# A KV-cache copy cut in two: half rows of 1,984 B in place of packets of 63 KB

## The chip, the cores and the metric

The kernel runs on one core of a Trainium2 chip. A core has five engines that run their own instruction streams: TensorE (PE, matmuls), VectorE (DVE), ScalarE (ACT), GpSimd (POOL) and SyncE (SP). Data moves between HBM and the on-chip memory, or within HBM, by DMA: an engine issues a transfer into its own queue, and sixteen DMA engines that all queues share carry it out. The metric is the time of one execution on the device, in microseconds (us).

## The reference

One layer of a decoder: 512 prompt tokens and 8 sequences of 4 new tokens each. A combined input projection feeds a convolution branch and an attention branch with three groups of key/value (KV) windows; then come an output projection, a layer norm, a feed-forward network (FFN) and a second layer norm. For the 8 sequences the reference also returns each group's KV window, moved on by 4 tokens:

```python
WINDOWS = (128, 512, 2048)
...
cat = jnp.concatenate([kv_prev[g].astype(kv_new.dtype), kv_new], axis=1)
o, lse = dilated_attn_sample(q, cat[:, :, 0], cat[:, :, 1], DILATIONS[g], slopes)
new_kv.append(cat[:, T:])
```

So 124 of 128, 508 of 512 and 2,044 of 2,048 old tokens of every sequence, 4 KB each, are copied from an input to an output without any arithmetic.

## The kernel before, in words

All activations are held with channels on the 128 partitions and the 544 tokens (512 and 32) along the row, in two halves of 272. Every projection is a stream of weight tiles: `load_more` (L109 to L117) has SP load a tile `wr` into one of four buffers, `prep_to` splits it into a high and a low part (a cast on ACT, L131, to `wh`, and a subtraction on DVE, L132, to `wl`), and `mm_group` (L189 to L200) runs three matmuls for each 128 channels and half (L194, L195, L197). The order of the instructions on each engine is the order in which the program writes them; other work (convolution, attention) is written as generators that `tick` advances between the matmul groups. SP is not held to that order by hand, but it too issues its transfers one after the other, and one that must wait holds all behind it.

The program goes through the first projections, four rounds of query/key/value projections (one for each pair of heads, `hp` 0 to 3), the gates with the branch projections, the output projection, and the FFN in three parts. The attention of a pair of heads lags a round behind its projections. Its last step, `combine_gen` (L554), turns a small table of softmax sums round through HBM: SP stores `st` to `dx` in HBM (L557, 8 KB, 128 pieces of 64 B) and loads it back as `stn` (L558). The load waits on SP until the store has landed.

At the start of the attention of the next pair, PE transposes the values into PSUM (`vtp`), ACT copies them out (`vT`, L473), and the score matmuls `S` (L486, L488) use the same PSUM buffers after that.

The KV copies are pieces in a list, `cp_pieces` (L167 to L178): for each sequence four pieces of the largest cache (out `s2`), one of the middle one (`s1`), and after every fourth sequence one piece for four sequences of the smallest (`s0`). ACT issues the next piece (L186) each time that `copies` has been called often enough: in the query/key/value rounds (L647) and in the first two and the third part of the FFN (L1073, L1079). These places in ACT's order are called slots here; what is left in the list is issued at L1099.

Transfers that SP and ACT issue take turns in the use of eight completion semaphores; an instruction that issues a transfer can therefore wait for an older one.

Of the kernel before, what the change touches and what calls it, by code (L numbers as in the profile page):

```python
# [54 lines left out]
def hybrid_step_kernel(ctx: ExitStack, tc: tile.TileContext, I, O):  # L55
# [33 lines left out]
    def C(name):  # L89
        o, w = CST[name]  # L90
        return cst[:, o:o + w]

    def big_tile(i, shape, dt, name):
        return big.tile(shape, dt, tag=f"L{i}", name=name)

    # ---------------------------------------------------------------- weight stream
    stream = []
    done = []
    pos = {"load": 0, "prep": 0, "use": 0, "free": 0}
# [58 lines left out]
        for m in range(8):  # L158
            add_w(I["w_down"][m, :, k0:k1, :], k1 - k0, None if j < 2 else (f"wd{m // 4}", f"wd{m // 4}", m % 4))

    # ---------------------------------------------------------------- background work
    bg = []

    def tick():
# [4 lines left out]
    cp_pieces = []  # L169
    for b in range(NB):  # L170
        for h in range(4):
            cp_pieces.append((O["s2"][b].rearrange("(p a) -> p a", p=128)[:, h * 4088:(h + 1) * 4088],
                              I["c2"][b, 4096:].rearrange("(p a) -> p a", p=128)[:, h * 4088:(h + 1) * 4088]))
        cp_pieces.append((O["s1"][b].rearrange("(p a) -> p a", p=128),
                          I["c1"][b, 4096:].rearrange("(p a) -> p a", p=128)))
        if b % 4 == 3:
            cp_pieces.append((O["s0"][b - 3:b + 1].rearrange("b (p a) -> b p a", p=128),
                              I["c0"][b - 3:b + 1, 4096:].rearrange("b (p a) -> b p a", p=128)))  # L178
    cp_acc = [0.0]

    def copies(n):
# [3 lines left out]
            o, i = cp_pieces.pop(0)  # L185
            act.dma_start(out=o, in_=i)  # L186

    # ---------------------------------------------------------------- matmul groups
    def mm_group(w, A, nk, halves=(0, 1)):  # L189
        hi, lo = w  # L190
        ps = {h: pmm.tile([128, 512], F32, tag="mm", name="mm") for h in halves}
        for k in range(nk):
            for h in halves:
                pe.matmul(ps[h][:, :HC], lhsT=hi[:, k], rhs=A[h][:, 0, k], start=(k == 0), stop=False)  # L194
                pe.matmul(ps[h][:, :HC], lhsT=hi[:, k], rhs=A[h][:, 1, k], start=False, stop=False)  # L195
            for h in halves:
                pe.matmul(ps[h][:, :HC], lhsT=lo[:, k], rhs=A[h][:, 0, k], start=False, stop=(k == nk - 1))  # L197
            if len(halves) == 2 and nk > 4 and k == nk // 2 - 1:
                tick()
        return ps  # L200

    # ---------------------------------------------------------------- setup
    ct = const.tile([128, 8, 9], F32, name="ct")
    csg = const.tile([128, 8, 9], F32, name="csg")
    cpad = const.tile([128, 8, 32], F32, name="cpad")
# [35 lines left out]
        act.copy(out=A[:, 0, ks, 240:], in_=src)  # L241
        dve.tensor_tensor(out=A[:, 1, ks, 240:], in0=src, in1=A[:, 0, ks, 240:].bitcast(F32), op=ALU.subtract)

    # ---------------------------------------------------------------- first modulation, u, first projections
    U = [big_tile(h, [128, 2, 8, HC], F32R, f"u{h}") for h in range(2)]

    def ada_mm(g):
# [61 lines left out]
    early_mm(2)  # L309
    dve.tensor_scalar(out=qb, in0=V("b_in", 0, 60), scalar1=0.125, scalar2=None, op0=ALU.mult)  # L310

    # ---------------------------------------------------------------- the other modulation parts
    aslots = (3, 4, 5, 6, 3, 4, 6, 4)
    abox = {}

# [36 lines left out]
                    out=modT[:, part, q0:q0 + 4, :], in0=pt[:, :, 32 * j:32 * j + 9],  # L352
                    scalar=0.0 if part == 3 else 1.0, in1=bias, op0=ALU.add, op1=ALU.add)

    # ---------------------------------------------------------------- GLU
    glu = big_tile(2, [128, 4 * 542 + 4 * NB * 34 + NS * CW], F32, "glu")
    glu_p = glu[:, :4 * 542].rearrange("p (c t) -> p c t", c=4)
    glu_s = glu[:, 4 * 542:4 * 542 + 4 * NB * 34].rearrange("p (c b t) -> p c b t", c=4, b=NB)
# [35 lines left out]
    pool.dma_start(out=O["conv_s"], in_=glu_s.rearrange("p c b t -> p (c b t)"))  # L394
    pool.dma_start(out=O["conv_p"], in_=glu_p[:, :, 512:542])

    # ---------------------------------------------------------------- layer norm (channel-major)
    def ln_core(z, nk, scratch, width, wait):
        acc = tmp.tile([128, HC], F32, tag="ln", name="lnacc")
        dve.tensor_reduce(out=acc, in_=z.rearrange("p k n -> p n k"), axis=AX.X, op=ALU.add)  # L400
        for _ in range(wait):
            yield
        ps = ps_o.tile([128, 512], F32, tag="o", name="lnps")
        pe.matmul(ps[:, :HC], lhsT=ones, rhs=acc, start=True, stop=True)
        mean = ps[:, :HC].unsqueeze(1).to_broadcast([128, 2, HC])
        for k in range(0, nk, 2):
            zz = z[:, k:k + 2]
            dve.scalar_tensor_tensor(out=zz, in0=mean, scalar=-1.0 / width, in1=zz, op0=ALU.mult, op1=ALU.add)
            act.activation(out=scratch[:, k:k + 2], in_=zz, func=AF.Square)
        acc2 = tmp.tile([128, HC], F32, tag="ln", name="lnacc2")  # L410
        dve.tensor_reduce(out=acc2, in_=scratch.rearrange("p k n -> p n k"), axis=AX.X, op=ALU.add)
        for _ in range(wait):
            yield
        ps2 = ps_o.tile([128, 512], F32, tag="o", name="lnps2")
        pe.matmul(ps2[:, :HC], lhsT=ones, rhs=acc2, start=True, stop=True)
        sd = tmp.tile([128, HC], F32, tag="ln", name="lnsd")
        act.activation(out=sd, in_=ps2[:, :HC], func=AF.Sqrt, scale=1.0 / width, bias=epst[:, 0:1])
        dve.reciprocal(out=sd, in_=sd)
        return sd

    # ---------------------------------------------------------------- conv branch
    box = {}

    def conv_gen():
# [35 lines left out]
            yield  # L460
        box["Y"] = [Y[:, 0], Y[:, 1]]

    # ---------------------------------------------------------------- prompt attention
    att = []
    dist = C("dist")

# [132 lines left out]
        split_rows(oa[:, HC:], att[1], hp, 0, 240)  # L599
        yield  # L600

    # ---------------------------------------------------------------- qkv projections
    conv = conv_gen()
    chain = []
    idle = [False]
# [48 lines left out]
    pool.dma_start(out=O["ks"], in_=smp[:, :, 3 * NS:])  # L654
    pool.dma_start(out=O["vs"], in_=smv.rearrange("p c b n -> p c (b n)"))

    # ---------------------------------------------------------------- decode attention
    dect = C("dect")

    live = {}  # L660
# [1 line left out]
    def load_k(b):  # L662
        KT = big_tile(5, [128, 9, 4, 132], F32, "KT")
        for g in range(3):
            sp.dma_start(out=KT[:, 3 * g:3 * g + 3], in_=I["kt"][b, :, 3 * g:3 * g + 3])
        live["k", b] = KT
# [110 lines left out]
        act.copy(out=att[1][:, 0, :, 240:], in_=as32)  # L777
        dve.tensor_tensor(out=att[1][:, 1, :, 240:], in0=as32, in1=att[1][:, 0, :, 240:].bitcast(F32), op=ALU.subtract)

    # ---------------------------------------------------------------- gates and branch projections  # L780
    load_k(0)
    chain.append(attn_gen(3, qk, 2, lambda: load_v(0), decode_gen))
    idle[0] = True
# [4 lines left out]
    for m in range(8):  # L788
# [5 lines left out]
        for h in range(2):  # L794
            hs = slice(h * HC, (h + 1) * HC)
# [30 lines left out]
    for m in range(8):  # L826
        ps = mm_group(w_next(), att, 4)
        mg = tmp.tile([128, NT], F32, tag="w", name="mg")
        for h in range(2):
            hs = slice(h * HC, (h + 1) * HC)  # L830
# [16 lines left out]
    for m in range(0, 8, 2):  # L847
        sp.dma_start(out=z[:, m:m + 2], in_=I["x_t"][:, m:m + 2])

    # ---------------------------------------------------------------- output projection, LN1, u2  # L850
    res["wo1"] = [big_tile(i, [128, 4, 8, 128], F32R, f"wo1{i}") for i in (2, 3)]
    flags.add("wo1")
    def bt(ap):
# [2 lines left out]
    u2 = {}  # L856
# [111 lines left out]
    for h in range(2):  # L968
        stats = Stats(h, dve if h else pool)
        for m in range(8):  # L970
# [12 lines left out]
            if h == 1:  # L983
                a = tmp.tile([128, NS], F32, tag="w", name="zsa")
# [12 lines left out]
        bg.append(ln1_gen(h, stats))  # L997
        tick()

    # ---------------------------------------------------------------- FFN  # L1000
    def gu_evict(pg, pu, Hs, fi):
        hs = list(pg)
        sg = {}
        for h in hs:
            sg[h] = tmp.tile([128, HC], F32, tag="w", name="sgf")
            act.activation(out=sg[h], in_=pg[h][:, :HC], func=AF.Sigmoid)
        for h in hs:
            dve.tensor_tensor(out=sg[h], in0=sg[h], in1=pg[h][:, :HC], op=ALU.mult)
        for h in hs:
            dve.tensor_tensor(out=sg[h], in0=sg[h], in1=pu[h][:, :HC], op=ALU.mult)  # L1010
        for h in hs:
            act.copy(out=Hs[h][:, 0, fi], in_=sg[h])  # L1012
        for h in hs:
            dve.tensor_tensor(out=Hs[h][:, 1, fi], in0=sg[h], in1=Hs[h][:, 0, fi].bitcast(F32), op=ALU.subtract)
# [25 lines left out]
    for j, (k0, k1) in enumerate(FF_CHUNKS):  # L1040
# [3 lines left out]
        if j == 0:  # L1044
            gw = [w_next(1) for _ in range(4)]
            first = []
# [191 lines left out]
```

## Time and profile before

| | |
|---|---|
| median of 3 runs | 1056.1 us |
| lowest, highest | 1054.32, 1061.54 us |
| profiled execution, from first to last instruction | 1060.8 us |
| PE busy | 1008.7 us, 95% of the span |
| data moved by DMA | 242.64 MB |
| of it by ACT's queue, mostly KV copies | 88.43 MB in 5,640 packets |
| copies issued by ACT | 32 of 2,044 KB, 8 of 2,032 KB, 2 of 1,984 KB |

The profile is one execution, traced on the chip; its own time is given as that span alone. It lies 4.7 us above the median of the runs. In the rows below, an instruction carries the line of the kernel that made it, and its names stand as out<-in. PE is a matmul, PEq, ACTq and SPq are an engine's instruction queue (there a transfer is issued). q1 is the DMA queue of SP, q10 that of ACT, q0 that of POOL. "[11.44 <-ACT vT L473]" means that the engine stood idle for 11.44 us before the instruction and that the named one ended the wait. PEclk is the granted clock of TensorE as a share of the full one.

### The profile page before, as it was taken

The numbers are of one execution on the slowest core, as the hardware profiler recorded it, in microseconds if no ns is written. First come the engines' busy times: TensorE is split into PE (matmuls) and PEld (weight loads), VectorE is DVE, ScalarE is ACT, GpSimd is POOL, SyncE is SP. The second block draws the span as 40 slices with busy tenths as digits, with TensorE's granted clock in tenths as the row PEclk, the third lists the DMA queues.
The fourth block names the chain that finished last, engine by engine and source line by source line (L and its number), as shares of the span: only waits on it lengthen the run. The fifth ranks groups of instructions, "written<-read, shape, count | busy, mean of one in ns | idle before, by whom it ended". The sixth has DMA issues, their size and how long they took to land.

```text
span 1060.8 us, 21530 instructions
## 1 busy us (share of the span) xinstructions
PE 1008.7 (95%) x9168; PEld 966.8 (91%) x9168; DVE 564.5 (53%) x988; ACT 415.9 (39%) x798; POOL 154.4 (15%) x226
## 2 busy tenths in 40 slices
PE   4999999999999959999999989999999999999995
PEld 3887999999988958999999989999999999999994
DVE  3422788789786335343216868633433434434487
ACT  3312235445448438544433445522212322223333
POOL 0201010010004400111103565100000000000046
PEclk8999999999999989999999999999999999999998
DMA  9898688796785664599953620457765677744202
GB/s 380 332 389 318 232 300 288 243 341 236 267 300 183 269 207 155 177 381 394 371 210 97 237 80 21 135 191 263 254 233 175 228 245 256 250 172 152 82 24 85
DMA packets 42951, 242.64 MB, mean 229 GB/s; under 512 B 7400, under 2 KB 8680, under 8 KB 35624
## 3 DMA queue, kind: packets, MB, share of 16 engines
q1 hardware_dynamic: 34592, 126.83, 33.8%
q10 hardware_dynamic: 5640, 88.43, 22.9%
q0 software_dynamic: 2624, 26.02, 6.1%
q8 instruction: 72, 1.18, 0.4%
q14 instruction: 23, 0.19, 0.0%
HBM read 231.36 MB, written 97.58 MB: 310 GB/s over the span
## 4 chain that ended last, share of the span: by engine, by line
PE 77%; DVE 8%; DMA 6%; POOL 3%; ACT 3%; issue 2%; ACTq 0%; DVEq 0%; SPq 0%; POOLq 0%
PE mm L194 22%; PE mm L195 22%; PE mm L197 21%; DMA dx<-st 3%; PE od L735 2%; PE Sd L700 2%; PE adaps L329 1%; DMA wr<-in_w_in 1%; DVE mrg L824 1%; PE pt L511 1%; POOL z L978 1%; DVE wl L132 1%; DMA wr<-in_w_pc 1%; DMA cst<-in_cst 1%; DVE z L1029 1%
## 5 line engine op out<-in xcount | busy, mean ns | idle before, releaser
L194 PE MATMUL mm<-u,wh 128*128 128x272 f32 x1528 | 419.7, 292 | 0.0
L195 PE MATMUL mm<-u,wh 128*128 128x272 f32 x1528 | 412.5, 288 | 0.0
L197 PE MATMUL mm<-u,wl 128*128 128x272 f32 x1528 | 317.9, 288 | 0.0
L194 PEld LDWEIGHTS mm<-u,wh 128*128 128x128 f32 x1528 | 288.0, 188 | 14.2 <-issue 11.0
L195 PEld LDWEIGHTS mm<-u,wh 128*128 128x128 f32 x1528 | 287.9, 188 | 0.2
L132 DVE TENSOR_TENSOR wl<-wr,wh 128x1024 fp32r<-128x1024 f32 (+2 forms) x132 | 155.3, 1178 | 171.4 <-ACT wh L131 171.4
L197 PEld LDWEIGHTS mm<-u,wl 128*128 128x128 f32 x1528 | 239.7, 188 | 0.0
L131 ACT CAST wh<-wr 128x1024 fp32r<-128x1024 f32 (+2 forms) x132 | 130.5, 991 | 178.2 <-PE mm L195 129.0
L434 DVE SCALAR_TENSOR_TENSOR convy<-glu,vec,convy 128x512 f32<-128x512 f32 x120 | 95.6, 797 | 2.5
L195 PE MATMUL mm<-h,wh 128*128 128x272 f32 x240 | 64.8, 288 | 0.0
L194 PE MATMUL mm<-h,wh 128*128 128x272 f32 x240 | 64.5, 287 | 0.0
L1012 ACT CAST h<-sgf 128x272 fp32r<-128x272 f32 x44 | 17.0, 420 | 103.2 <-DVE sgf L1010 103.2
L894 POOL TENSOR_TENSOR lnq<-lnq,lnsq 128x272 f32<-128x272 f32 x4 | 3.1, 775 | 365.7 <-ACT lnsq L868 365.7
L1019 DVE SCALAR_TENSOR_TENSOR z<-mm,modT,z 128x272 f32<-128x272 f32 (+1 forms) x48 | 21.7, 479 | 55.4 <-PE mm L197 55.4
L1010 DVE TENSOR_TENSOR sgf<-sgf,mm 128x272 f32<-128x272 f32 x44 | 17.5, 434 | 63.3 <-PE mm L197 63.0
L197 PE MATMUL mm<-h,wl 128*128 128x272 f32 x240 | 49.6, 288 | 0.0
L632 ACT ACTIVATE qk<-mm,vec 128x272 f32<-128x272 f32 (+1 forms) x48 | 25.8, 625 | 56.6 <-PE mm L197 56.6
L194 PEld LDWEIGHTS mm<-h,wh 128*128 128x128 f32 x240 | 45.2, 188 | 0.0
L195 PEld LDWEIGHTS mm<-h,wh 128*128 128x128 f32 x240 | 45.2, 188 | 0.0
L504 ACT ACTIVATE P<-P,st 128x256 f32<-128x256 f32 x64 | 31.2, 489 | 28.6 <-DVE st L498 25.7
L195 PE MATMUL mm<-mrg,wo 128*128 128x272 f32 x128 | 37.8, 295 | 1.8 <-DVE mrg L824 1.7
L194 PE MATMUL mm<-mrg,wo 128*128 128x272 f32 x128 | 38.3, 300 | 0.0
(270 smaller groups left out, 1632.2 us busy)
## 6 DMA issues: line engine op xcount, KB each, us to landing
out_s<-in_c ACTq DMA_DIRECT2D x32, 2044.0 KB, 9.0
wr<-in_w_in SPq DMA_DIRECT2D x60, 512.0 KB, 6.3
wr<-in_w_gu SPq DMA_DIRECT2D x44, 512.0 KB, 4.3
KT<-in_kt SPq DMA_DIRECT2D x24, 792.0 KB, 7.5
VV<-in_vv SPq DMA_DIRECT2D x24, 768.0 KB, 7.4
gb<-in_w_ada POOLq DMA_DIRECT2D x8, 2048.0 KB, 16.8
out_s<-in_c ACTq DMA_DIRECT2D x8, 2032.0 KB, 8.9
ga<-in_w_ada SPq DMA_DIRECT2D x8, 1024.0 KB, 12.0
```

Source lines behind the costliest of these rows:

```text
L131: act.copy(out=hv, in_=raw)
L132: dve.tensor_tensor(out=lv, in0=raw, in1=hv.bitcast(F32), op=ALU.subtract)
L194: pe.matmul(ps[h][:, :HC], lhsT=hi[:, k], rhs=A[h][:, 0, k], start=(k == 0), stop=False)
L195: pe.matmul(ps[h][:, :HC], lhsT=hi[:, k], rhs=A[h][:, 1, k], start=False, stop=False)
L197: pe.matmul(ps[h][:, :HC], lhsT=lo[:, k], rhs=A[h][:, 0, k], start=False, stop=(k == nk - 1))
L434: dve.scalar_tensor_tensor(out=o, in0=src, scalar=sc, in1=o, op0=ALU.mult, op1=ALU.add)
L504: act.activation(out=p[:, a:b], in_=p[:, a:b], func=AF.Exp, bias=st[:, kd, s, hh, 0:1], accum_out=st[:, kd, s, hh, 1:2])
L632: act.activation(out=o, in_=src, func=AF.Identity, bias=V("b_in", col))
L700: pe.matmul(S[32 * c:32 * c + 32, 132 * g:132 * g + 132], lhsT=q[:, col:col + 32], rhs=KT[:, j, c], start=(t == 0), stop=(j == 0 or t == 3))
L735: pe.matmul(o[32 * c:32 * c + 32, :], lhsT=lhsT, rhs=rhs, start=(j == 0), stop=(j == 9))
L1010: dve.tensor_tensor(out=sg[h], in0=sg[h], in1=pu[h][:, :HC], op=ALU.mult)
L1019: dve.scalar_tensor_tensor(out=zz[:, :n1], in0=ps[:, :n1], scalar=modT[:, 5, m, 0:1], in1=zz[:, :n1], op0=ALU.mult, op1=ALU.add)
```

## The change

The piece for four sequences of the smallest cache becomes two pieces. Each sequence's 124 tokens are seen as 128 rows of 992 numbers (3,968 B); the first piece copies the first 496 numbers of each row (1,984 B), the second the rest. Nothing else in the program changes (the diff also empties some comment lines, and moves the later lines down by two).

```diff
         if b % 4 == 3:
-            cp_pieces.append((O["s0"][b - 3:b + 1].rearrange("b (p a) -> b p a", p=128),
-                              I["c0"][b - 3:b + 1, 4096:].rearrange("b (p a) -> b p a", p=128)))
+            for h in range(2):
+                hs = slice(h * 496, (h + 1) * 496)
+                cp_pieces.append((O["s0"][b - 3:b + 1].rearrange("b (p a) -> b p a", p=128)[:, :, hs],
+                                  I["c0"][b - 3:b + 1, 4096:].rearrange("b (p a) -> b p a", p=128)[:, :, hs]))
```

The list has 44 pieces in place of 42. Three places of ACT's order show what that moves. A row is line, operation, out<-in and shape; `out_s0`, `out_s1` and `out_s2` are the copies, and the shape of a copy is the pattern of its destination, slowest count first, in numbers of 4 B. The tiles `qk3` are the projections of the last pair of heads, `P` and `PT` its attention, `convy` and `yconv` the convolution.

In the last round of projections, ACT before the change:

```order
L630 ACTIVATE qk3_3135<-mm_3618,qb_100 128x68x4
L630 ACTIVATE qk3_3135<-mm_3619,qb_100 128x60x4
L186 DMA out_s0<-in_c0 4x8x15872
L514 COPY PT_3712<-pt_3707 128x512
L409 ACTIVATE convy_1064<-convy_1064 128x2x272 x2
L131 CAST wh_3722<-wr_3331 128x1024
```

and with the change:

```order
L632 ACTIVATE qk3_3135<-mm_3618,qb_100 128x68x4
L632 ACTIVATE qk3_3135<-mm_3619,qb_100 128x60x4
L188 DMA out_s0<-in_c0 512x1x496
L516 COPY PT_3712<-pt_3707 128x512
L411 ACTIVATE convy_1064<-convy_1064 128x2x272 x2
L131 CAST wh_3722<-wr_3331 128x1024
```

The first copy of the smallest cache, 4 x 8 runs of 15,872 numbers, becomes its first half, 512 runs of 496, in the same slot.

The next two slots, at the end of that round and into the gates, before:

```order
L630 ACTIVATE qk3_3135<-mm_3809,qb_100 128x272
L630 ACTIVATE qk3_3135<-mm_3810,qb_100 128x240
L186 DMA out_s2<-in_c2 128x4088
L455 ACT_TABLE_LOAD
L455 ACTIVATE convy_1064<-convy_1064 128x4x272
L131 CAST wh_3877<-wr_3545 128x512
L534 COPY osb_3505<-o_3909 128x2x128
L458 CAST yconv_3241<-convy_1064 128x1088
L632 ACTIVATE qk3_3135<-mm_3883,vec_95 128x272
L632 ACTIVATE qk3_3135<-mm_3884,vec_95 128x240
L186 DMA out_s2<-in_c2 128x4088
L131 CAST wh_3961<-wr_3616 128x1024
```

and with the change:

```order
L632 ACTIVATE qk3_3135<-mm_3809,qb_100 128x272
L632 ACTIVATE qk3_3135<-mm_3810,qb_100 128x240
L188 DMA out_s0<-in_c0 512x1x496
L457 ACT_TABLE_LOAD
L457 ACTIVATE convy_1064<-convy_1064 128x4x272
L131 CAST wh_3877<-wr_3545 128x512
L536 COPY osb_3505<-o_3909 128x2x128
L460 CAST yconv_3241<-convy_1064 128x1088
L634 ACTIVATE qk3_3135<-mm_3883,vec_95 128x272
L634 ACTIVATE qk3_3135<-mm_3884,vec_95 128x240
L188 DMA out_s2<-in_c2 128x4088
L131 CAST wh_3961<-wr_3616 128x1024
```

The second half takes the slot of a copy of the largest cache; that copy moves to the next slot, and each later piece by one slot. Behind the second of these slots stand the cast of a weight tile and then the `vT` copies.

In the third part of the FFN (`sgf`, `h20`, `h21` are its activations), before:

```order
L1012 CAST h21_10200<-sgf_10564 128x272
L186 DMA out_s0<-in_c0 4x8x15872
L131 CAST wh_10575<-wr_10329 128x1024
L131 CAST wh_10631<-wr_10385 128x1024
L1006 ACTIVATE sgf_10687<-mm_10581 128x272
L1006 ACTIVATE sgf_10689<-mm_10582 128x272
L1012 CAST h20_10199<-sgf_10687 128x272
L1012 CAST h21_10200<-sgf_10689 128x272
L131 CAST wh_10699<-wr_10454 128x1024
```

and with the change:

```order
L1014 CAST h21_10200<-sgf_10564 128x272
L188 DMA out_s1<-in_c1 32x16256
L131 CAST wh_10575<-wr_10329 128x1024
L131 CAST wh_10631<-wr_10385 128x1024
L1008 ACTIVATE sgf_10687<-mm_10581 128x272
L1008 ACTIVATE sgf_10689<-mm_10582 128x272
L1014 CAST h20_10199<-sgf_10687 128x272
L1014 CAST h21_10200<-sgf_10689 128x272
L188 DMA out_s0<-in_c0 512x1x496
```

The list now ends two slots later: the last copy of the smallest cache stood in the first of these slots, where now the last of the middle cache stands; its halves stand in the second of these slots and in the one after it.

## Rows read from the trace of the kernel before

**Rows 1.** Of the page, part 1: busy time, share of span, instructions

```profile
PE 1008.7 (95%) x9168; PEld 966.8 (91%) x9168; DVE 564.5 (53%) x988; ACT 415.9 (39%) x798; POOL 154.4 (15%) x226
```

**Rows 2.** Waits of all engines, whole span: who, for whom, us, times, longest

```profile
PE S L486 <- ACT vT L473: 11.4, 1, 11.4
...
PE adaps L251 <- DVE cpad L228: 6.7, 1, 6.7
```

**Rows 3.** Chain that ended last, 336 to 400 us: start, us, what

```profile
343.72 37.12 DMA dx<-st
...
381.33 7.87 DMA wr<-in_w_pc
389.21 0.63 ACT wh L131
```

**Rows 4.** Waits of SP's queue, whole span

```profile
SPq L558 <- DMA dx<-st: 42.3, 4, 36.6
```

**Rows 5.** Tile dx, whole span: time to landing

```profile
DMA to landing us min/median/max: 1.4/3.0/37.1
```

**Rows 6.** SP in order of time, 335 to 395 us: start, us, what

```profile
342.96 0.66 SPq L115 DMA_DIRECT2D wr<-in_w_in  x1
343.72 0.43 SPq L557 DMA_DIRECT2D dx<-st  x1
380.86 0.38 SPq L558 DMA_DIRECT2D stn<-dx  x1
```

**Rows 7.** ACT in order of time, 336 to 398 us

```profile
342.14 1.19 ACTq L186 DMA_DIRECT2D out_s<-in_c  x1
...
356.13 0.56 ACTq L186 DMA_DIRECT2D out_s<-in_c  x1
...
363.56 0.83 ACT L632 ACTIVATE qk<-mm,vec 128x272 f32<-128x272 f32 x2
...
380.01 1.04 ACT L131 CAST wh<-wr 128x1024 fp32r<-128x1024 f32 x1 [15.62 <-DMA wr<-in_w_in]
380.96 1.55 ACT L473 COPY vT<-vtp 128x512 f32<-128x512 f32 x3
```

**Rows 8.** PE in order of time, 366 to 403 us

```profile
382.08 1.49 PE L486 MATMUL S<-qk 64*128 64x128 f32 x7 [11.44 <-ACT vT L473]
```

**Rows 9.** Stretches: window, length, PE busy (count), granted clock, DMA share, GB/s

```profile
370.60:382.00 11.40, 0.04 (x1) 0.73 0.46 171
382.00:386.00 4.00, 3.92 (x20) 0.50 1.02 399
386.00:390.00 4.00, 4.00 (x34) 0.99 0.87 256
```

**Rows 10.** DMA queues, 352 to 356 us: packets, MB, share of 16 engines

```profile
q10 hardware_dynamic: 5, 0.32, 18.3%
q1 hardware_dynamic: 5, 0.03, 1.5%
```

**Rows 11.** DMA queues, 359.4 to 362.5 us

```profile
q10 hardware_dynamic: 60, 1.22, 102.1%
```

**Rows 12.** DMA packets by size, 349 to 352 us

```profile
DMA packets 234, 0.91 MB, mean 304 GB/s; under 512 B 127, under 2 KB 127, under 8 KB 226
```

**Rows 13.** DMA packets by size, 377 to 380.5 us

```profile
DMA packets 107, 0.27 MB, mean 77 GB/s; under 512 B 52, under 2 KB 52, under 8 KB 102
```

**Rows 14.** DMA queues, first 22 us

```profile
q10 hardware_dynamic: 576, 0.74, 9.2%
```

**Rows 15.** Of the page, part 3: queue totals

```profile
q1 hardware_dynamic: 34592, 126.83, 33.8%
```

**Rows 16.** The same, around the second copy of the smallest cache

```profile
955.00:980.00 25.00, 25.00 (x201) 1.00 0.44 159
```

**Rows 17.** PE's waits, 670 to 1020 us

```profile
PE mm L194 <- DVE sgf L1008: 0.5, 1, 0.5
```

## The prediction

> **What bounds the kernel now.** I read the totals first. TensorE (PE) is busy for 1008.7 of 1060.8 us [rows 1], so a copy between two places in HBM can matter only where it makes PE stop. The list of waits says where that is: PE's longest single wait in the whole program is 11.4 us, before the matmuls of L486 [rows 2]. Next the chain of work that ended last, in that stretch: it holds one piece of 37.12 us, the small transfer dx<-st, then a load of w_pc, then a cast on ACT [rows 3]. SP's own list agrees: of the 42.3 us that SP waited for dx in four rounds, 36.6 are one round [rows 4], while the same 8 KB transfer takes 3.0 us in the median [rows 5].
>
> In order of time: SP issues a weight tile from w_in at 342.96 and dx at 343.72, and can issue nothing, stn least of all, until 380.86 [rows 6]. ACT issues copies at 342.14 and 356.13, is done with its other work at 364.39 (363.56 + 0.83), and then waits until 380.01 for that weight tile; the vT copies stand behind this cast [rows 7]. PE runs out at 370.64 and resumes at 382.08 [rows 8]. It resumes on a granted clock of 0.50, the lower of its two levels (1.2 GHz), and the full one is back at about 386; it had idled for 11.4 us before [rows 9].
>
> What keeps an 8 KB transfer for 37 us? The copy issued at 342.14 is the first copy of the smallest cache. Its pattern is 4x8x15872 elements: 32 packets of 63,488 B. From 352 to 356 us the ACT queue (q10) shows 5 packets, 0.32 MB, in 18.3% of sixteen engines' time: 0.183 x 16 x 4 / 5 = 2.34 us a packet. SP's queue (q1) got exactly 5 packets through beside them [rows 10]. So the copy moves 80 GB/s there, about three packets at a time, against 1.22 MB in 3.1 us (394 GB/s) once the next copy, of 16,352 B packets, runs as well [rows 11]: it sits on a few of the sixteen DMA engines, I take it four (its slowest count), eight packets each, 18.7 us of work. On these four the weight tile, the KT loads before it and dx pass one packet at a time between packets of 2.34 us, and later between the other copies. The small packets show it: most of dx's 128 pieces are among the 127 of 349 to 352 us [rows 12], but a second batch of small packets comes at 377 to 380.5 us [rows 13], just before SP goes on. Twelve engines were done by 352; four were 28 us late.
>
> **The change part by part.** Removed: the 63,488 B packets. Added: per copy twice 512 packets of 1,984 B, with a slowest count of 512, so that I spread them over sixteen engines, 32 each. A packet of this size between HBM and HBM is not in the trace. Nearest rows: in the first 22 us q10 moved 576 packets, 0.74 MB, in 9.2%: 0.056 us for 1,285 B, in proportion 0.087 us for 1,984 B [rows 14]; the mean q1 packet, of 3.7 KB, costs 0.338 x 16 x 1060.8 / 34592 = 0.166 us [rows 15]. The far end is a 16 KB copy packet: (1.021 x 16 x 3.1 - 2 x 3) / 58 = 0.77 us, two 63 KB packets of at most 3 us taken off [rows 11]. I take 0.087, since its packets are nearest in size; the ends are 0.056 and 0.77.
>
> *The stall.* A half copy then adds 32 x 0.087 = 2.8 us to each engine, whatever the order in which the queues take turns. The undisturbed engines had weight tile and dx through by 352, so both land by about 352 + 2.8 = 355. They are needed when ACT casts: cast 1.04 and vT copies 1.55 [rows 7] must end by 370.64, so the tile has until 368.0, 13 us later. The wait of 11.44 us goes [rows 8]. The clock no longer falls there: from 382 to 386 PE was busy 3.92 us at 0.50 [rows 9], work of 1.96 us at 1.00, so 1.96 more. Sum: 13.4 us.
>
> *What is late next.* SP can issue stn and the w_pc tile at about 355 instead of 381. That tile landed 7.87 us after its issue [rows 3], so at 363; ACT cast it 7.1 us after PE resumed (389.21 against 382.08), which becomes 370.6 + 7.1 = 377.7. There are 14 us to spare, and the copy at ACT's third slot, of the larger cache as before, stands behind the same cast.
>
> *The second half and the shift.* At ACT's slot of 356.13 the second half replaces a 16,352 B copy, and less data moves there than before. Issuing costs ACT some 0.5 us at either slot (0.56 there; the first took 1.19) [rows 7]; ACT has 15.6 us of idle time behind it. From there on each piece moves back by one slot, and at the end by two: the last two slots, empty before, fall into the third part of the FFN. I cost that at nothing, because the second copy of the smallest cache ran there from about 955 to 980 with the large packets and PE stayed busy 25.00 of 25 us [rows 16], and from 670 to 1020 PE waited for a total of 0.5 us [rows 17]. Its packets are now smaller, so its cover grows; the other pieces keep their packets. If the cover were gone, a stop like the one removed would cost the same 13.4 us.
>
> *Sum.* Profiled execution: 1060.8 - 13.4 = 1047.4. The page gives its span alone; the median of the runs is 4.7 us lower, and I subtract the same 13.4 from it: 1056.1 - 13.4 = **1042.7 us**.
>
> **The rivals.**
> (1) The stop is shorter without the profiler. The 4.7 us between the profiled span and the median must lie somewhere; if all of it is in this wait, the gain is 8.7 and the time 1047.4. For: landing of dx depends on how queues happen to interleave. Against: eight packets of 2.34 us are there in any run, and there are other waits for loads, at the start, to hold 4.7 us.
> (2) Small packets are dear. At p us a packet the tile lands at 352 + 32p and PE resumes 2.6 us later (1.04 + 1.55), so the stop comes back above p = 0.5. At the far end, 0.77, the tile lands at 376.6 instead of 379.5, and the time is 1056.1 - 2.9 = 1053.2. From p = 0.86 the kernel is **slower** than before, from 1.19 by over 1% (1066.7). Against: 1.19 is 14 times what 0.087 says; packets of 1,285 B went at 0.056 [rows 14].
> (3) Another wait steps in between 370 and 400 us, where loads, stores from the qk tiles and a copy meet: the w_pc wait or a later DVE turn takes back 3 to 9 us, 1046 to 1051, say 1049. Against: the 14 us to spare above.
> (4) It is only one transfer cut in two, and the time stays 1056.1. The Trainium skill, page "DMA: Bandwidth & Descriptors", section "Rules for kernel authors", says that two transfers to disjoint halves are not worth it, as both spray over the same sixteen engines and serialize, and that one large transfer is better. By that rule nothing is won here; but the trace has the old copy on few engines, so its premise does not hold [rows 10, 11].
> (5) The change doesn't spread: the halves stay on four engines, 128 packets each. Then each q1 packet there waits 0.087 us instead of 2.34, and the copy adds at most 128 x 0.087 = 11.1 us: everything lands by 363, before 368.0, and the time is again 1042.7. So the forecast rests on the packets' size or on the spread, and either will do.
>
> **How the numbers follow.** About 1% (10.6 us) is what a measurement of this kernel can tell from no change; its three runs lie 7.2 us apart. Chances: forecast, with (5), 0.63; (1) 0.17; (2) 0.08, of it 0.03 slower by over 1%; (3) 0.07; (4) 0.05. The forecast lies below 1045.5, the others but for the tail of (2) within 1%: faster 0.63, same 0.34, slower 0.03. The range goes down to 1038, for the spread of the runs below their median (1.8) and a few us more should DVE and ACT, no longer bunched up after the stop, run smoother; up to 1051, which takes in (1) and (3) and leaves out (4) and nearly all of (2), 0.13.
>
> **What would show it.** Right: dx lands within some 12 us at the third round too; SP's longest wait for it falls from 36.6 to about 10; the wait of L486 for vT is gone and the granted clock stays at 1.00 from 370 to 390; q10 has 64 packets fewer and 2,048 more; PE still never waits in the FFN. Wrong: a wait of L486 that stays near 11 us with dx landing early (then dx was not the cause), 1,984 B packets of over 0.5 us, or a new PE wait after 670.

## The result, and the profile after

The changed kernel takes 1047.08 us in the median of 4 runs (1046.5 to 1048.44); the kernel before, timed beside it, 1058.82 us (4 runs, 1054.32 to 1062.77). The ratio of the runs is 0.9878 (that of the two medians 0.9889), with a 95% interval of 0.9849 to 0.9908: faster by about 1.2%. The range of the prediction held the time, and the direction and the place of the gain were right; the price of 1042.7 us was 4.4 us too low.

The profiled execution has a span of 1046.4 us, 14.4 us shorter than before. Its page, part 1 (busy time, share, instructions), against [rows 1]:

```profile
PE 1006.8 (96%) x9168; PEld 964.8 (92%) x9168; DVE 564.4 (54%) x988; ACT 416.1 (40%) x798; POOL 153.4 (15%) x226
```

PE does the same matmuls in 1006.8 us. Its list of waits now begins elsewhere; the 11.4 us of L486 [rows 2] are gone. Who, for whom, total, times, longest:

```profile
PE adaps L253 <- DVE cpad L230: 6.9, 1, 6.9
PE adaps L253 <- DMA ga<-in_w_ada: 5.9, 2, 5.4
PE fb L594 <- DVE P L498: 2.9, 4, 1.2
```

These stand at the start of the program (`adaps`) and, four times under 1.3 us, in the attention's last step (`fb`). The tile dx lands within 9.8 us even in its worst round, against 37.1 [rows 5]:

```profile
DMA to landing us min/median/max: 1.4/3.6/9.8
```

SP in order of time, against [rows 6]: the load back follows the store after 9.8 us, and the next weight tile goes out at 354.21 in place of 381.33.

```profile
343.12 0.70 SPq L115 DMA_DIRECT2D wr<-in_w_in  x1
343.92 0.39 SPq L559 DMA_DIRECT2D dx<-st  x1
353.74 0.38 SPq L560 DMA_DIRECT2D stn<-dx  x1
354.21 0.46 SPq L115 DMA_DIRECT2D wr<-in_w_pc  x1
```

ACT in order of time, against [rows 7]. The halves are issued at 342.26 and 356.30. The cast that had waited for its tile until 380.01 now runs at 365.92, and the vT copies are done at 368.54, before PE needs them:

```profile
342.26 1.22 ACTq L188 DMA_DIRECT2D out_s<-in_c  x1
...
356.30 0.68 ACTq L188 DMA_DIRECT2D out_s<-in_c  x1
...
363.54 2.34 ACTq L188 DMA_DIRECT2D out_s<-in_c  x1
...
365.92 1.06 ACT L131 CAST wh<-wr 128x1024 fp32r<-128x1024 f32 x1 [1.36 <-issue]
366.98 1.56 ACT L475 COPY vT<-vtp 128x512 f32<-128x512 f32 x3
...
374.74 0.60 ACT L131 CAST wh<-wr 128x512 fp32r<-128x512 f32 x1
```

One thing in it is new: the issue in the third slot takes 2.34 us, and ACT stands idle for 1.36 us behind it. PE, which came to the score matmuls at 370.64 and got 382.08 before [rows 8], runs them at 370.74, with no idle time in front:

```profile
370.74 0.72 PE L488 MATMUL S<-qk 64*128 64x128 f32 x8
```

Nor does the clock fall. The stretches after this point (window, length, PE busy with count, granted clock, DMA share, GB/s) have 1.00, where [rows 9] had 0.73 and 0.50:

```profile
370.70:382.00 11.30, 11.30 (x98) 1.00 0.93 365
382.00:386.00 4.00, 3.49 (x30) 1.00 0.62 213
386.00:390.00 4.00, 3.52 (x34) 1.00 0.08 31
```

To see where the 14.4 us went, I cut both profiles at matching places, by nearly the same count of matmuls. After:

```profile
340.00:400.00 60.00, 58.49 (x499) 1.00 0.60 215
400.00:570.00 170.00, 169.83 (x2288) 1.00 0.73 273
```

and before:

```profile
340.00:414.40 74.40, 60.59 (x498) 0.93 0.56 201
414.40:584.40 170.00, 169.83 (x2290) 1.00 0.73 273
```

From 340 on the same work takes 60.0 us in place of 74.4, and in the stretches that follow PE's busy time is alike to the hundredth. So the whole difference lies there: 11.44 us of wait; 60.59 - 58.49 = 2.1 us that PE was busy longer, at the lower clock; and the rest of 0.9 us in the waits for DVE before `fb` (1.4 us before, 0.5 after).

What the copy itself does now is not what I had thought. The DMA packets by size and the DMA queues from 357.5 to 359.9 us, with the halves running (packets, MB, share of sixteen engines):

```profile
DMA packets 263, 0.33 MB, mean 139 GB/s; under 512 B 124, under 2 KB 236, under 8 KB 263
q10 hardware_dynamic: 112, 0.22, 24.2%
q1 hardware_dynamic: 151, 0.11, 14.3%
```

112 packets in 0.242 x 16 x 2.4 us are 0.083 us each, and 0.242 x 16 = 3.9 engines are busy with them all the time: the halves still sit on **four** engines. The trace's landing events say the same: after the issue, the first half's completion semaphore gets four of them (361.4 to 362.6 us), that of the weight tile issued at 343.12 sixteen. But beside the copy's 112 packets SP's queue moved 151, among them 112 pieces of 16 B of `stn`: one for each packet of the copy, as in [rows 10], where 5 of SP's went through beside 5 large ones in a longer time. In all, ACT's queue has 7,632 packets in place of 5,640 for the same 88.43 MB.

### The profile page after: what moved, and what is told of

It reads as the page before. It is cut to its first block, busy times and chain, and to the rows that moved or that the text cites. A ratio compares the mean times of both kernels' runs of the same rounds, so it can differ in the third digit from the quotient of the medians.

```text
span 1046.4 us, 21532 instructions
## 1 busy us (share of the span) xinstructions
PE 1006.8 (96%) x9168; PEld 964.8 (92%) x9168; DVE 564.4 (54%) x988; ACT 416.1 (40%) x798; POOL 153.4 (15%) x226
## 3 DMA queue, kind: packets, MB, share of 16 engines
q10 hardware_dynamic: 7632, 88.43, 23.2%
## 4 chain that ended last, share of the span: by engine, by line
PE 78%; DVE 10%; ACT 5%; POOL 3%; issue 2%; DMA 2%; ACTq 0%; DVEq 0%; POOLq 0%
PE mm L196 23%; PE mm L197 22%; PE mm L199 22%; PE od L737 2%; PE Sd L702 2%; PE adaps L331 1%; DVE mrg L826 1%; DMA wr<-in_w_in 1%; PE pt L513 1%; DVE wl L132 1%; DMA cst<-in_cst 1%; PE o L529 1%; DVE z L1031 1%; DVE lns L878 1%; DVE P L498 1%
## 6 DMA issues: line engine op xcount, KB each, us to landing
gb<-in_w_ada POOLq DMA_DIRECT2D x8, 2048.0 KB, 16.7
```

## The experiments

Two theories stood against each other. **Turns**: on an engine that a copy uses, each packet of SP's queue waits for one packet of the copy, so that a short transfer is late by as many copy packets as it has packets queued, times their length. **Spread**: what harms is that a copy sits on four engines. Beside them I tried whether the cut into two, the slot, or the shift of the later pieces gives the gain. The kernel before, timed beside the first four runs, took 1061.32 us (8 runs), and beside the last four 1061.52 us (7 runs). All edits are to the kernel before; where a diff only adds lines that append pieces, they stand in place of the two lines that the first diff removes.

**The same packets on eight engines, and half as long ones on sixteen.**

```diff
-            cp_pieces.append((O["s0"][b - 3:b + 1].rearrange("b (p a) -> b p a", p=128),
-                              I["c0"][b - 3:b + 1, 4096:].rearrange("b (p a) -> b p a", p=128)))
+            cp_pieces.append((O["s0"][b - 3:b + 1].rearrange("b (p a) -> p b a", p=8),
+                              I["c0"][b - 3:b + 1, 4096:].rearrange("b (p a) -> p b a", p=8)))
```

> One transfer as before, with the same 63,488 B packets, on eight DMA engines in place of four, four packets on each. Theory 'turns' (on an engine that the copy uses, each packet of SP's queue waits for one copy packet, so the delay is the number of copy packets on an engine times their length): four turns of 2.34 us, 9.4 us in all, so the weight tile lands by about 362, dx within about 18 us, and PE does not wait at L486 (under 1 us). Rival 'size' (packets of 63 KB on SP's way are bad in any number): the wait of L486 stays above 8 us. Time under 'turns' about 1047, under 'size' about 1058.

One run took 1045.21 us. The queue of ACT from 345 to 349 us shows the large packets on 0.471 x 16 = 7.5 engines:

```profile
q10 hardware_dynamic: 12, 0.76, 47.1%
```

SP's longest wait for dx is 17.3 us (total of four rounds, times, longest), in place of 36.6 [rows 4]; from 340 to 402 us PE waits for nothing over 0.5 us.

```profile
SPq L558 <- DMA dx<-st: 23.5, 4, 17.3
```

The second kernel has p=16 in the same two lines, and thus sixteen engines and 31,744 B.

> One transfer, 31,744 B packets, on all sixteen engines, four on each; the slots of all other pieces are those of before. 'Turns': four turns of about 1.2 us, 4.7 us in all; dx lands within 14 us, no wait at L486, a time of 1045 to 1049, as with the change. 'Small packets are needed': part of the wait stays, over 3 us, and the time is above 1051.

1046.85 us (4 runs), ratio 0.9863 (0.9848 to 0.9877); dx landed after 15.2 us at worst, where 14 at most were expected, and the longest wait for it, of 14.7 us, is over before PE needs anything behind it:

```profile
SPq L558 <- DMA dx<-st: 21.9, 4, 14.7
```

So neither small packets nor a cut is needed: four turns on each engine in place of eight, of 63,488 or of 31,744 B, do as well as the change. "Size" falls.

**Both halves in one slot.** The rows of 1,984 B stay, and so do the four engines, but no other piece moves.

```diff
+            pair = ()
+            for h in range(2):
+                hs = slice(h * 496, (h + 1) * 496)
+                pair += (O["s0"][b - 3:b + 1].rearrange("b (p a) -> b p a", p=128)[:, :, hs],
+                         I["c0"][b - 3:b + 1, 4096:].rearrange("b (p a) -> b p a", p=128)[:, :, hs])
+            cp_pieces.append(pair)
...
-            o, i = cp_pieces.pop(0)
-            act.dma_start(out=o, in_=i)
+            p = cp_pieces.pop(0)
+            for j in range(0, len(p), 2):
+                act.dma_start(out=p[j], in_=p[j + 1])
```

> Both halves (1,984 B packets) issued one behind the other in the old slot; no other piece moves. 'Turns': 256 packets of 0.085 us on each of four engines, 21.8 us of copying, but an SP packet waits 0.085 us at a time: dx lands within 13 us, no wait at L486, 1045 to 1049. 'Cut' (what helped is that half the data moved to a later slot): the four engines are busy as long as before, so dx takes over 25 us and the wait stays above 5 us, time above 1052. 'Shift' (the later pieces' new slots brought the gain): time stays at 1056 or more.

1057.98 us (5 runs), ratio 0.9971 (0.9956 to 0.9985). The time is that of a failure, yet what "turns" says of dx came true: it lands within 9.7 us at worst.

```profile
DMA to landing us min/median/max: 1.5/2.0/9.7
```

L486 no longer waits either. A new wait has taken its place, which none of the three theories had named. ACT in order of time: the issue of the second half lasts 9.56 us, and behind it ACT stands idle for 9.01 us, with no other instruction to blame ("issue").

```profile
341.90 9.56 ACTq L191 DMA_DIRECT2D out_s<-in_c  x1
...
351.56 0.59 ACT L519 COPY PT<-pt 128x512 f32<-128x512 f32 x1 [9.01 <-issue]
```

PE then waits for the copy out of PSUM that stands behind it (total, times, longest), and its clock falls again; from 345 to 361 us it is 0.68 in the mean, with 9.26 us busy of 16:

```profile
PE o L532 <- ACT PT L519: 6.3, 1, 6.3
```

```profile
345.00:361.00 16.00, 9.26 (x50) 0.68 0.49 175
```

When the issue ends, at 351.46, ACT's queue has moved 133 packets, 33 of the 128 that the first half has for each of four engines:

```profile
q10 hardware_dynamic: 133, 0.26, 9.3%
```

So it looked as if the queue takes only some 90 to 95 packets for an engine ahead, and holds the engine that issues more. Two later runs test this.

**Two halves of whole packets.** Cut like the change and in the same slots, but each half is the first or second 63,488 numbers of each sequence, four packets of 63,488 B on each of four engines.

```diff
+            for h in range(2):
+                hs = slice(h * 63488, (h + 1) * 63488)
+                cp_pieces.append((O["s0"][b - 3:b + 1, hs].rearrange("b (p a) -> b p a", p=4),
+                                  I["c0"][b - 3:b + 1, 4096:][:, hs].rearrange("b (p a) -> b p a", p=4)))
```

> Cut in two like the change and issued in the same slots, but each half is four whole packets of 63,488 B per engine, on four engines. 'Turns': four turns of 2.34 us in the first slot and four more from 357 on, when some 20 SP packets are still queued on each of the four engines: the tile lands at about 368, dx takes 24 to 27 us, PE waits 0 to 3 us at L486. 'Cut': as good as the change, dx within 12 us and no wait. 'Size' alone: wait above 8 us.

One run: 1055.27 us. dx was out of the way sooner than I had worked out, after 16.7 us, and L486 does not wait: the second half, issued at 354.34, moves its first packet at 357.7 in the trace, when dx has all but landed. But stn, issued at 358.34, meets the second half. SP in order of time, and stn's time to landing:

```profile
341.65 0.40 SPq L559 DMA_DIRECT2D dx<-st  x1
358.34 0.38 SPq L560 DMA_DIRECT2D stn<-dx  x1
358.81 0.46 SPq L115 DMA_DIRECT2D wr<-in_w_pc  x1
```

```profile
DMA to landing us min/median/max: 2.2/11.9/21.6
```

Of its four rounds the slowest took 21.6 us, and the weight tile issued at 358.81 stands behind it: ACT's cast waits for that until 380.35, and PE for 7.1 us before `fb`.

```profile
380.35 0.62 ACT L131 CAST wh<-wr 128x512 fp32r<-128x512 f32 x1 [7.48 <-DMA wr<-in_w_pc]
```

```profile
PE fb L594 <- DVE P L498: 7.4, 2, 7.1
```

The cut alone moves the stop from the first transfer to the next one in SP's queue. stn is cut into 512 pieces of 16 B, 32 for an engine, and by "turns" each of them waits for a packet of a copy, here of the second half until 367.6 us and then of the copy in the third slot. That I had not counted.

**The first copy moved out of the way.**

```diff
+    cp_pieces.insert(23, cp_pieces.pop(20))
     cp_acc = [0.0]
```

> The copies are those of before, packets of 63,488 B on four engines; only the first copy of the smallest cache trades places with three copies of the largest cache and is issued at about 670, as the first of the FFN. 'Turns': its large packets hurt only where short transfers wait on SP's queue with PE close behind; so dx lands within 14 us, there is no wait at L486, PE waits for nothing over 1 us in the FFN, and the time is 1045 to 1049. Rival 'any copy in that slot': a wait at L486 of over 5 us stays.

1047.65 us (4 runs), ratio 0.9879 (0.9844 to 0.9915). dx lands within 13.6 us, and in the FFN, where both copies with large packets now run, PE waits at most 0.5 us:

```profile
DMA to landing us min/median/max: 1.4/3.1/13.6
```

```profile
PE mm L195 <- DVE sgf L1009: 0.5, 1, 0.5
```

**The large copy doubled.**

```diff
+    cp_pieces.insert(21, cp_pieces.pop(41))
     cp_acc = [0.0]
```

> The second copy of the smallest cache is issued right behind the first, in the slot of 356, in place of a copy of the largest one. 'Turns': sixteen large packets on each of the four engines, some 38 us from 346 on; of the 25 SP packets that queue there, the weight tile's last is about the 17th and lands at 384 to 390, dx after 390. The wait of L486 grows from 11.4 to 15 to 22 us, and the time to 1066 to 1082. Rival 'the large copy is not what holds the tile': the wait stays at 11 us and the time near 1061.

1073.61 us in one run. ACT's cast runs at 391.12, PE's wait at the score matmuls is 24.1 us in place of 11.4, and SP waits 49.5 us for dx:

```profile
391.12 1.04 ACT L131 CAST wh<-wr 128x1024 fp32r<-128x1024 f32 x1 [28.29 <-DMA wr<-in_w_in]
```

```profile
PE S L487 <- ACT vT L474: 24.1, 1, 24.1
```

```profile
SPq L559 <- DMA dx<-st: 55.0, 4, 49.5
```

The tile landed at about 390.5, where 384 to 390 was expected; PE's wait is 2 us over the range given for it. Taking the large packets away and doubling them move the stop as "turns" says.

**Both halves in one slot once more, with fewer packets on an engine.** First spread (`p b a` in place of `b p a`): 32 packets of 1,984 B on each of sixteen engines.

> Both halves (1,984 B packets) in one slot as in the earlier run with the pair, but spread over all sixteen engines, 32 packets of each half on an engine. In that earlier run the issue of the second half held ACT for 9.6 us. If that was a queue that takes only some 90 packets on an engine ahead of the transfer (theory 'depth'), it now takes under 1.5 us, nothing waits over 1 us between 340 and 400, and the time is 1045 to 1049. If any second issue in a slot holds ACT (rival 'second issue', by a semaphore that an older transfer still holds), ACT is held for 8 us or more and the time is 1056 to 1060 again.

1047.34 us (4 runs), ratio 0.9883 (0.9846 to 0.9919). The second issue takes 0.61 us:

```profile
341.89 0.61 ACTq L191 DMA_DIRECT2D out_s<-in_c  x1
```

Then on four engines again, with rows of 3,968 B (p=64, halves of 992 numbers), 64 packets on each for a half:

> Both halves in one slot on four engines, as in the earlier run with the pair, but with rows of 3,968 B: 64 packets on an engine per half in place of 128. 'Depth' (some 90 packets): the second issue takes under 2 us; 'turns': an SP packet waits 0.16 us at a time, so the tile and dx land in time; no wait over 1.5 us between 340 and 400 and 1045 to 1050. 'Second issue': 8 us or more on ACT, 1056 to 1060. 'Spread' (four engines are the harm, whatever the packets): dx takes over 20 us and the time is above 1052.

1046.92 us (4 runs), ratio 0.9875 (0.9833 to 0.9916). The second issue takes 0.67 us, and the next slot, where some 94 of the 128 packets are still left on each engine, 1.76 us:

```profile
342.05 0.67 ACTq L191 DMA_DIRECT2D out_s<-in_c  x1
...
354.79 1.76 ACTq L191 DMA_DIRECT2D out_s<-in_c  x1
```

This is the run that the one with the pair was meant to be: four engines, nothing shifted, and the whole gain. "Spread" and "shift" fall with it, and "second issue" with both. The issues that were held (9.56 us with the first pair, 2.34 us in the third slot of the change, 1.76 us) were let go when the traces have some 95, 90 and 82 packets left on each engine, and one with 71 in front of it, in the next slot of the first pair, was not held (0.58 us). So a queue that takes some 80 to 95 packets of an engine ahead agrees with all of them; the figure was not measured any closer, and why it is so stays open.

No version beats the change clear of noise: the medians of the kernels without a stop (for the eight engines a single run) lie between 1045.2 and 1047.7 us, and runs of one and the same kernel lie up to 2.7 us apart (1046.76 to 1049.46).

## Why the prediction was right

*The place and the mechanism.* As predicted, the stop before L486 hung on the first copy of the smallest cache, whose packets SP's transfers had to let pass one by one. Moved away, it is gone; doubled, it grows from 11.4 to 24.1 us. The landing events show it engine by engine: before, twelve of the weight tile's sixteen had come by 352.3 us and the other four at 377.8 to 379.4; with the change the last is there at 352.9.

*The size of the gain.* 13.4 us were predicted, and the two profiles differ by 14.4: 11.44 of wait as priced, 2.1 for the clock where 1.96 stood in the sum, and 0.9 at `fb` that I had left to the range ("run smoother").

*The step that failed: the spread.* "I spread them over sixteen engines, 32 each" is wrong. I read the count of 512 from the destination; in the source each sequence begins 131,072 numbers after the one before, so its slowest count stays 4. The trace has 3.9 engines busy. The Trainium skill, page "DMA: Bandwidth & Descriptors", section "Why a DMA increments its semaphore by 16 and not by 1", says that the engines are the largest number up to 16 that divides the slowest counts of both sides, which gives 4 here; the trace agrees. So the case that came true is rival (5), to which the prediction gave the same time: packets of 0.083 us (0.087 was the estimate) let SP's queue through even on four engines. The weight tile and dx were expected by 355; they landed at 352.9 and 353.7.

*The step that was mis-sized: the time it is taken from.* I subtracted from a median of 1056.1 us of three runs, and took the profiled execution to be 4.7 us slower than that. But a run's time is some 2 us above its span (1048.44 and 1046.4 for the profiled execution after), so that of the profiled one before is 1062.8; less 13.4 that gives 1049.4, against 1048.44 measured. In the later comparisons the kernel before has a median of 1061.3 and 1061.5, some 14.3 us above the changed one; in the first it is 11.7 above, since two of its four runs there are low ones. Rival (1) named 1047.4, close to the result, but its reason, a stop that is shorter without the profiler, does not hold for most runs: of 19 runs of the kernel before, 16 lie between 1060.0 and 1063.0, where the profiled one does. The other three, at 1053.9 to 1056.1, may have had a shorter stop; none of them left a trace, and this stays open.

*What I had costed at nothing* cost nothing. The w_pc tile landed at 362.2 and was cast at 374.74, behind other work of ACT and not behind its load. In the FFN, PE's longest wait is still 0.5 us, as in [rows 17]:

```profile
PE mm L196 <- DVE sgf L1010: 0.5, 1, 0.5
```

*The third slot* was misread. The prediction has its copy behind the cast of the weight tile, but in ACT's order it stands in front. Before the change its issue, too, stood until the tile landed (342.96 + 36.5), whose completion semaphore it uses next in the trace, and its 0.52 us are part of the 11.44:

```profile
DMA to landing us min/median/max: 36.5/36.5/36.5
379.45 0.52 ACTq L186 DMA_DIRECT2D out_s<-in_c  x1
```

With the change it took 2.34 us, where the sum had put nothing (and 0.5 at each of the first two, which took 1.22 and 0.68). ACT had the time. With both halves in one slot it had not, and that took back nearly the whole gain.

*The other rivals.* (2) Small packets are not dear, 0.083 us. (3) Nothing stepped in at this place; in the run with whole packets in two halves just that happened. (4) "Only one transfer cut in two" is wrong in that the time moved, and the cut with whole packets shows what it does by itself: the stop moves on to stn.

## What to carry to other kernels

Where a small transfer takes ten times as long as its like, look at which copies run then, on how many engines (here four, by the slowest count of the source, though the destination had 512) and in packets of what length: what waited behind it here paid one such packet for each of its own. Shorter packets, a wider spread and another place in the order each cured it here, and each is worth only what the engine behind the late transfer loses. Putting very many packets on a few engines had a price of its own, at the engine that issued the next transfer: 9.56 us behind 128 on each of four.

## What the runs showed of the hardware that I had not expected

An issue of a transfer, else 0.5 to 1.2 us, held ACT for 9.56 us until only 95 of the 128 packets of the one before were left on each engine; with 32 or 64 packets it took 0.61 and 0.67. A load of 8 KB in 512 pieces took up to 21.6 us beside copies of packets of 63,488 and 16,352 B, in place of 7.1 us at most (4.8 in the median) in the changed kernel. And an idle stretch of 24.1 us was followed, like the one of 11.4, by matmuls at the granted clock of 0.50, here from 393 to 399 us of the run with the doubled copy:

```profile
393.00:399.00 6.00, 5.80 (x28) 0.50 0.92 334
```
